# Spatial gate's value rows projected in one pass of 512 columns, with weights loaded two inner tiles at a time and split by VectorE

## The chip, the cores and the metric

The kernel runs on one core of one Trainium2 chip. The time is device microseconds (us) of that core from launch to end; the median of three runs is quoted, and one more execution was recorded by the hardware profiler. PE is the matrix engine (TensorE), DVE is VectorE, ACT is ScalarE, POOL is GpSimd, SP is the engine that issues most loads.

## What is computed

One layer of a diffusion backbone over 1,280 tokens (1,024 latent and 256 context) of width 1,024. A modulated RMSNorm `u` of the tokens is projected by `w_in` into the inputs of three branches (pooling, spatial gating, a bidirectional mLSTM with four heads) and their gates; the gated branches are merged, projected out, and a feed-forward part follows. The change touches the branch with the spatial gate:

```python
proj = u @ w_in
xp, su, sv, q, k, v, o_pre, gate_pre, br_pre = jnp.split(proj, points, axis=-1)
y_b = sgu_branch(su, sv, g_sgu, w_sgu, b_sgu)

def sgu_branch(u, v, g_sgu, w_sgu, b_sgu):
    B, T, _ = u.shape
    vn = rmsnorm(v, g_sgu).reshape(B, T // CHUNK, CHUNK, N_SGU_GROUPS, SGU_GROUP)
    mixed = jnp.einsum('gpq,bnqgc->bnpgc', w_sgu, vn) + jnp.swapaxes(b_sgu, 0, 1)[None, None, :, :, None]
    return u * mixed.reshape(B, T, D_SGU)
```

`sv` (1,280 rows of 512 columns) is `u` times 512 columns of `w_in`; each row is normalised by its own root mean square over the 512 columns.

## The kernel before

**Matrix products.** Every operand is held as two rounded parts, `hi` and `lo` (`hi` is a rounded copy made by ACT, `lo` is the rest, made by a subtraction), and a product is three matmuls: hi·hi, lo·hi, hi·lo. `uT[k][g]` holds the transposed `u` for inner tile k (8 tiles of 128) and token group g (512, 512 and 256 tokens).

**The spatial rows (`sv`, lines 685 to 707).** For these, tokens are the output rows: the stationary operand is 128 tokens of `uT`, the moving operand is the weight. The 512 columns are done in two halves `q` of 256. For each half, `load_w` fetches two tiles `[128, 1024]` (four inner tiles by 256 columns each), ACT rounds them (line 93) and, with `eng=G`, POOL subtracts (line 94). Then ten token tiles `i` follow, each 8 × 3 matmuls of 256 columns into half of a bank `ps_mm`; ACT copies the result into `vn[i]` (line 701) and takes its sum of squares (line 702) into `vsq`. After both halves the two sums are added (line 704), `rstd_of` makes the inverse root (a DVE and a POOL instruction, lines 129 and 130), and DVE scales the ten `vn` (line 707).

**What stands around it.** A scheduler orders all instructions by its own estimate of time; the engines then run their queues in that order. In that order the `sv` matmuls lie between the steps of the last two heads of the mLSTM (`head(2)`, `head(3)`): a head's group of chunks goes through `st` and `rb` (lines 627, 631), DVE and ACT build the weights `w` and `e` (lines 635 to 645), PE multiplies them into `pv` (lines 654, 656), ACT and DVE normalise (lines 659 to 670) and PE transposes back (`th`, line 671). Groups are numbered 0, 1, 2 within a head. Each head's output gate `p_o` uses the same three banks `ps_mm` as `sv` and is read out by ACT on line 617.

**After `sv`** come the pooling branch and the rest of the spatial branch: `pool_project` (`p_xp`), `pool_window` (sums over windows on DVE and POOL, lines 758 to 776, in regions of the tile `z` that the last head uses until its `pv` is done), `pool_out` (`pp`, line 783), and `spatial(ci)`: ten matmuls `mx` of `vn` (line 831), `mt` on DVE (line 835), a projection `p_su`, and the product of both on DVE (line 842), which is what frees a bank of `p_su`.

**Pools.** `raw` has 2 buffers of `[128, 1024]`, `hi` and `lo` 3 each (`NRAW`, `NHL`), `ps_mm` 3 banks, `ps_sd` 5 banks, `slot` 59 tiles of `[128, 512]`.

Of the kernel before, what the change touches and what calls it, by code (L numbers as in the profile page):

```python
# [7 lines left out]
F32 = mybir.dt.float32  # L8
F32R = mybir.dt.float32r
AF = mybir.ActivationFunctionType  # L10
ALU = mybir.AluOpType
# [3 lines left out]
P = 128  # L15
D = 1024
KT = D // P
NSAMP = 1024
T = 1280
NT = T // P  # L20
# [8 lines left out]
NTMP, NRAW, NHL = 5, 2, 3  # L29
# [19 lines left out]
def hybrid_step(  # L49
# [8 lines left out]
    V, A, G, PE = engines  # L58
# [6 lines left out]
    wp = pw.enter_context(tc.tile_pool(name="wp", bufs=NRAW))  # L65
# [3 lines left out]
    def slot(name, dt=F32R):  # L69
        return sp.tile([P, 512], dt, tag="s", name=name)  # L70
# [4 lines left out]
    def ps_mm(name):  # L75
        return pp.tile([P, 512], F32, tag="mm", name=name, bufs=3)
# [4 lines left out]
    def small(shape, name, bufs=4):  # L81
        return cp.tile(shape, F32, tag=f"sm{shape[-1]}", name=name, bufs=bufs)

    def fetch_w(src, name):
        raw = wp.tile([P, 1024], F32, tag="raw", name=f"raw_{name}")
        SP.dma_start(raw, src)
        return raw

    def load_w(src, name, raw=None, eng=V):
        raw = fetch_w(src, name) if raw is None else raw  # L90
        hi = wp.tile([P, 1024], F32R, tag="hi", name=f"hi_{name}", bufs=NHL)
        lo = wp.tile([P, 1024], F32R, tag="lo", name=f"lo_{name}", bufs=NHL)
        A.copy(hi, raw)
        eng.tensor_tensor(lo, raw, hi.bitcast(F32), ALU.subtract)
        return hi, lo
# [10 lines left out]
    def split_part(name, g):  # L106
        if g < 2:
            return slot(f"{name}h{g}"), slot(f"{name}l{g}")
        c = slot(f"{name}c")
        return c[:, 0:256], c[:, 256:512]  # L110
# [16 lines left out]
    def rstd_of(ssq, n, name):  # L127
        r = small([P, 16], f"rs_{name}")
        V.tensor_scalar(r[:, :n], ssq, 1.0 / n_of[name[0]], EPS, ALU.mult, ALU.add)  # L129
        G.tensor_tensor(r[:, :n], r[:, :n], neghalf[:, :n], ALU.pow)  # L130
        return r
# [89 lines left out]
    uT = [[] for _ in range(KT)]  # L221
# [54 lines left out]
    V, A, G, PE = (Pinned(tc, e) for e in engines)  # L276
# [119 lines left out]
    for at, (g, k) in enumerate(steps):  # L396
# [3 lines left out]
        if (g, k) == (1, 2):  # L400
# [4 lines left out]
            for i in range(2):  # L405
                w = slot(f"wgs{i}").rearrange("p (k c) -> p k c", c=P)
# [25 lines left out]
    V, A, G, PE = engines  # L432
# [251 lines left out]

    vn = []
    vsq = cp.tile([P, NT, 2], F32, name="vsq")
    for q in range(2):
        wq = [load_w(w_sv[q, hf], f"sv{q}_{hf}", eng=G) for hf in range(2)]
        for i in range(NT):
            g, o = (i * P) // 512, (i * P) % 512  # L690
            if q == 0:
                vn.append(slot(f"vn{i}", F32))
            ps = ps_mm(f"sv{q}_{i}")
            for k in range(KT):
                whi, wlo = wq[k // 4]
                s = slice((k % 4) * 256, (k % 4 + 1) * 256)
                uh, ul = uT[k][g]
                PE.matmul(ps[:, :256], uh[:, o : o + P], whi[:, s], start=k == 0, stop=False)
                PE.matmul(ps[:, :256], ul[:, o : o + P], whi[:, s], start=False, stop=False)
                PE.matmul(ps[:, :256], uh[:, o : o + P], wlo[:, s], start=False, stop=k == KT - 1)  # L700
            A.copy(vn[i][:, q * 256 : (q + 1) * 256], ps[:, :256])
            A.activation(ps[:, 256:512], ps[:, :256], AF.Square, accum_out=vsq[:, i, q : q + 1])
    vs1 = small([P, 16], "vs1")[:, :NT]
    V.reduce_sum(vs1, vsq, axis=mybir.AxisListType.X)
    r = rstd_of(vs1, NT, "v")
    for i in range(NT):
        V.tensor_scalar(vn[i], vn[i], r[:, i : i + 1], None, ALU.mult)
# [179 lines left out]
    def tmp2(name, dt=F32):  # L887
        return q1.tile([P, 512], dt, tag="s", name=name, bufs=6)
# [156 lines left out]
    for ri, r in enumerate(ORDER):  # L1045
        scr = (scr_ya, scr_yb, scr_yc)[r]
        ys = [[] for _ in range(4)]
        for g in range(3):
            for kc in range(4):
                t0, n = GROUPS[g]  # L1050
                raw = tmp2(f"yr{r}_{kc}_{g}")
                SP.dma_start(raw[:, :n], scr[kc, :, t0 : t0 + n])
                hi, lo = split_part(f"y{r}_{kc}", g)
# [3 lines left out]
        for d in range(KT):  # L1057
            if d % 2 == 0:
                wb = [load_half(w_branch[r, d // 2][:, i * 512 : i * 512 + 512], f"wb{r}_{d}_{i}") for i in range(2)]
            for g in range(3):  # L1060
# [4 lines left out]
                for kc in range(4):  # L1065
                    yh, yl = ys[kc][g]
                    whi, wlo = wb[kc // 2]
                    o = kc % 2 * 256 + (d % 2) * P
                    s = slice(o, o + P)
# [230 lines left out]
    for j in range(2):  # L1300
        for hf in range(2):
            t = q2.tile([P, 512], F32, name=f"gt2{j}{hf}")
# [152 lines left out]
def _layout(inputs):  # L1455
    import numpy as np

    f = {k: np.asarray(v) for k, v in inputs.items()}
    a = {}
    a["xs"] = np.concatenate([f["x_sample"][0], f["x_prompt"][0]], 0).reshape(NT, P, D)  # L1460

    def col(v, n):
        return v.reshape(n, P).T

    cond = np.stack([f["c"][0], f["c_ctx"]], -1).reshape(KT, P, 2).transpose(1, 0, 2).reshape(P, 16)
    a["cols"] = np.concatenate(
        [
            cond, col(f["b_ada"][0, :2048], 16), col(f["g_norm1"][0], 8), col(f["g_norm2"][0], 8),
            col(f["pool_scale"][0], 4), col(f["g_sgu"][0], 4), col(f["g_mlstm"][0], 4),
        ], 1)  # L1470
    s = np.arange(P)
    neg = np.float32(-1e30)
    a["consts"] = np.concatenate(
        [
            np.eye(P, dtype=np.float32),
            np.where(s[:, None] <= s[None, :], np.float32(0), neg),
            np.where(s[:, None] >= s[None, :], np.float32(0), neg),
            np.tile(np.eye(2, dtype=np.float32), (64, 1)),
        ], 1).astype(np.float32)
    sel = np.zeros((100, 8), np.float32)  # L1480
    for d in range(2):
        for h in range(H):
            sel[32 * d + h, 4 * d + h] = 1.0
            sel[64 + 32 * d + h, 4 * d + h] = 1.0
    a["sel8"] = sel
    a["w_ada"] = f["w_ada"][0]
    a["b_ada"] = f["b_ada"]
    w = f["w_in"][0]
    wd = np.concatenate([w[:, :1024], w[:, 1536:3584], w[:, 3600:]], 1)
    a["w_in"] = wd.reshape(KT, P, 48, P).transpose(2, 1, 0, 3).reshape(48, P, KT * P)  # L1490
    a["w_sv"] = w[:, 1024:1536].reshape(2, 4, P, 2, 256).transpose(3, 0, 2, 1, 4).reshape(2, 2, P, 1024)
    wgt = np.zeros((KT, P, P), np.float32)
    wk = w[:, 3584:3600].reshape(KT, P, 16)
    bg = np.zeros((36, 2), np.float32)
    m0 = np.zeros((36, 1), np.float32)
    for t in range(2):
        for d in range(2):
            j = t * 8 + d * 4
            for o in (0, 4):
                wgt[:, :, 64 * t + 32 * d + o : 64 * t + 32 * d + o + 4] = wk[:, :, j : j + 4]  # L1500
            bg[32 * d : 32 * d + 4, t] = f["b_gates"][0, j : j + 4]
    for d in range(2):
        m0[32 * d : 32 * d + 4, 0] = f["state_m"][0, 0, d]
    a["w_gate"] = wgt.transpose(1, 0, 2)
    a["bg"], a["m0"] = bg, m0
    a["w_branch"] = f["w_branch"][0].reshape(3, 4, P, 4, 256).transpose(0, 3, 2, 1, 4).reshape(3, 4, P, 1024)
    a["w_out"] = f["w_out"][0].reshape(KT, P, 2, 512).transpose(2, 0, 1, 3)
    a["w_ff1"] = f["w_ff1"][0].reshape(KT, P, NFF, P).transpose(2, 1, 0, 3).reshape(NFF, P, D)
    a["w_ff2"] = f["w_ff2"][0].reshape(NFF, P, D)
    a["w_pool"] = f["w_pool"][0].transpose(1, 0, 2)  # L1510
    a["w_sgu"] = f["w_sgu"][0].transpose(2, 0, 1)
    a["b_sgu"] = f["b_sgu"][0].reshape(1, 4 * P)

    def inv(n, win):
        t = np.arange(n)
        cnt = np.clip(t + win - win // 2, 0, n) - np.clip(t - win // 2, 0, n)
        return (np.float32(1.0) / cnt.astype(np.float32)).astype(np.float32)

    a["pcnt"] = np.stack([
        np.concatenate([np.outer(inv(GRID_H, w_), inv(GRID_W, w_)).ravel(), inv(256, w_)]) for w_ in POOL_WINDOWS])  # L1520
    st = np.concatenate([f["state_C"][0, 0], f["state_n"][0, 0][..., None]], -1)
    a["state"] = st.transpose(1, 2, 0, 3)
    a["gfin"] = f["g_final"].reshape(1, D)
    return {k: np.ascontiguousarray(v) for k, v in a.items()}
# [31 lines left out]
```

## Time and profile before

| | us |
|---|---|
| median of three runs (lowest, highest) | 1944.16 (1943.91, 1946.34) |
| the profiled execution's own time | 1943.31 |
| its span, first to last instruction | 1941.3 |
| PE busy | 1908.4 (98%) |
| DVE busy | 1287.9 (66%) |
| ACT busy | 856.7 (44%) |
| POOL busy | 382.1 (20%) |

The span is what the trace covers; the time adds what lies around it. Busy shares are means over the whole span. A PE that counts as busy can still be slower than it could be, since matmuls overlap and what counts is the distance from one start to the next. Where PE is idle, the views name the engine and line that released it.

### The profile page before, as it was taken

Reading aid. Unit: us, or ns where it says so; the run is one execution under the profiler, and the core shown is the slowest. Engines: PE = TensorE matmul, PEld = TensorE weight load, DVE = VectorE, ACT = ScalarE, POOL = GpSimd, SP = SyncE. Lnnn points to the kernel's source line nnn. Section 1 sums busy time; section 2 is a strip of 40 time slices with the busy share of each in tenths; the row PEclk is TensorE's granted clock in tenths of the full one; section 3 lists DMA queues with packets and bytes.
Section 4 is the critical chain, followed back from the end, with each engine's and each line's share of the span. In section 5 each row is a group of like instructions: output and inputs, shape, how many; then the busy total and the mean of one; then the engine's idle time right before and its main releaser. Section 6 shows DMA issues by size and latency. Waiting matters only on the chain.

```text
span 1941.3 us, 28162 instructions
## 1 busy us (share of the span) xinstructions
PE 1908.4 (98%) x10166; PEld 1632.5 (84%) x10166; DVE 1287.9 (66%) x2200; ACT 856.7 (44%) x1760; POOL 382.1 (20%) x381
## 2 busy tenths in 40 slices
PE   8999999999999999999999999999999999999998
PEld 5878888998788888888888888888888888888886
DVE  6574443447759899875675599887876655754665
ACT  6444454653243333343123375555454544443443
POOL 1100001108202424230000005554431210000003
PEclk9999999999999999999999999999999999999999
DMA  9210111012635445459532435777774596654444
GB/s 370 77 60 33 45 38 39 28 57 68 204 125 168 151 151 161 157 195 328 164 103 98 151 121 200 275 263 264 250 256 139 193 335 203 210 168 152 165 133 160
DMA packets 149318, 313.33 MB, mean 161 GB/s; under 512 B 17550, under 2 KB 40818, under 8 KB 147130
## 3 DMA queue, kind: packets, MB, share of 16 engines
q1 hardware_dynamic: 107354, 220.73, 34.6%
q0 software_dynamic: 15520, 57.75, 7.8%
q10 hardware_dynamic: 26304, 33.04, 4.7%
q8 instruction: 80, 1.31, 0.3%
q14 instruction: 60, 0.49, 0.1%
HBM read 217.59 MB, written 93.36 MB: 160 GB/s over the span
## 4 chain that ended last, share of the span: by engine, by line
PE 87%; DVE 6%; ACT 2%; issue 2%; DMA 2%; POOL 1%; SPq 0%; ACTq 0%; POOLq 0%; DVEq 0%
PE w L1423 6%; PE w L1424 6%; PE w L1425 6%; PE fT L912 3%; PE fT L910 3%; PE fT L911 3%; PE pb L1071 3%; PE pb L1070 3%; PE pb L1072 3%; PE fB L911 2%; PE fB L910 2%; PE fB L912 2%; PE fT_g L912 2%; PE fT_g L910 2%; PE fT_g L911 2%; PE po L1190 2%
## 5 line engine op out<-in xcount | busy, mean ns | idle before, releaser
L1262 POOL TENSOR_TENSOR z<-z 128x512 f32<-128x512 f32 x64 | 100.6, 1572 | 119.6 <-DMA z<-in_w_ff 110.1
L967 DVE TENSOR_TENSOR z<-z 128x512 f32<-128x512 f32 x112 | 94.2, 841 | 2.5
L547 POOL PARTITION_ALL_REDUCE acc<-acc x16 | 54.4, 3435 | 183.4 <-DVE acc L541 114.3
L541 DVE SCALAR_TENSOR_TENSOR acc<-z,scond,acc 128x512 f32<-128x512 f32 x112 | 84.6, 803 | 0.1
L1377 POOL TENSOR_TENSOR rs_y<-rs_y,neghalf 128x1 f32<-128x1 f32 x10 | 9.7, 967 | 332.2 <-DVE rs_y L1376 332.1
L1228 ACT ACTIVATE z<-z 128x512 f32<-128x512 f32 x64 | 40.5, 632 | 75.7 <-DVE z L976 38.4
L992 ACT ACTIVATE z<-z 128x512 f32<-128x512 f32 x48 | 30.3, 632 | 54.2 <-DVE z L976 20.6
L130 POOL TENSOR_TENSOR rs_h<-rs_h,neghalf 128x4 f32<-128x4 f32 (+1 forms) x12 | 10.9, 909 | 200.0 <-DVE rs_h L129 199.8
L673 DVE SCALAR_TENSOR_TENSOR yc<-th,ccol,z 128x512 f32<-128x512 f32 (+1 forms) x12 | 7.9, 661 | 58.4 <-PE th L671 58.4
L1076 DVE TENSOR_TENSOR sg<-pb,sg 128x512 f32<-128x512 f32 (+1 forms) x48 | 28.8, 601 | 26.6 <-PE pb L1072 26.4
L901 ACT CAST hi_wb<-raw_wb 128x512 fp32r<-128x512 f32 x24 | 14.7, 620 | 64.0 <-PE pb L1071 37.9
L1229 ACT ACTIVATE z<-z 128x512 f32<-128x512 f32 x64 | 40.3, 629 | 1.1
L1191 DVE TENSOR_TENSOR po<-po,gt 128x512 f32<-128x512 f32 (+1 forms) x24 | 14.6, 609 | 35.6 <-PE po L1190 31.2
L548 POOL TENSOR_TENSOR acc<-acc,bt 1x512 f32<-1x512 f32 x16 | 26.2, 1651 | 59.1 <-issue 59.1
L1253 POOL DMA_DIRECT2D scr_s<-x x48 | 26.3, 550 | 52.4 <-DVE x L1247 46.6
L758 POOL TENSOR_TENSOR z<-z 128x1024 f32<-128x1024 f32 (+13 forms) x20 | 33.6, 1702 | 7.7 <-ACT z L742 5.4
L1194 ACT ACTIVATE po<-z 128x512 f32<-128x512 f32 (+1 forms) x24 | 12.7, 530 | 48.6 <-DVE z L1193 34.3
L607 DVE SCALAR_TENSOR_TENSOR z<-z,dmb,kv 128x129 f32<-128x129 f32 x56 | 16.6, 345 | 21.8 <-PE kv L596 21.3
L1077 DVE TENSOR_TENSOR z<-z,sg 128x512 f32<-128x512 f32 (+1 forms) x48 | 28.7, 602 | 1.2
L660 DVE TENSOR_TENSOR den<-den,gcol 128x2 f32<-128x2 f32 x40 | 6.2, 160 | 31.0 <-ACT den L659 29.9
L130 POOL TENSOR_TENSOR rs_f<-rs_f,neghalf 128x4 f32<-128x4 f32 (+1 forms) x3 | 3.3, 1092 | 116.9 <-DVE rs_f L129 116.9
L654 PE MATMUL pv<-z,w 128*128 128x129 f32 x160 | 25.1, 275 | 0.9 <-DVE w L638 0.9
(5142 smaller groups left out, 7274.1 us busy)
## 6 DMA issues: line engine op xcount, KB each, us to landing
z<-in_w_ff SPq DMA_DIRECT2D x64, 512.0 KB, 5.3
z<-in_w_ada SPq DMA_DIRECT2D x64, 256.0 KB, 3.4
scr_t<-z POOLq DMA_DIRECT2D x16, 1024.0 KB, 4.3
z<-in_w_in SPq DMA_DIRECT2D x24, 512.0 KB, 4.3
scr_g<-z ACTq DMA_DIRECT2D x48, 256.0 KB, 2.0
sg<-scr_g SPq DMA_DIRECT2D x48, 256.0 KB, 4.5
scr_h<-z ACTq DMA_DIRECT2D x48, 256.0 KB, 3.5
scr_s<-x POOLq DMA_DIRECT2D x48, 256.0 KB, 3.8
```

The costliest lines, as they stand in the source:

```text
L541: V.scalar_tensor_tensor(acc[j], raw, scond[:, k, j : j + 1], acc[j], ALU.mult, ALU.add)
L910: PE.matmul(ps, whi[:, s], ahi, start=first and k == ks[0], stop=False)
L911: PE.matmul(ps, whi[:, s], alo, start=False, stop=False)
L912: PE.matmul(ps, wlo[:, s], ahi, start=False, stop=end and k == ks[-1])
L967: V.tensor_tensor(out, x, y, op)
L1070: PE.matmul(pb[:, :n], whi[:, s], yh, start=kc == 0, stop=False)
L1071: PE.matmul(pb[:, :n], whi[:, s], yl, start=False, stop=False)
L1072: PE.matmul(pb[:, :n], wlo[:, s], yh, start=False, stop=kc == 3)
L1262: G.tensor_tensor(out, x, y, ALU.subtract)
L1423: PE.matmul(banks[j], h_[:, s], rh, start=fp == 0, stop=False)
L1424: PE.matmul(banks[j], l_[:, s], rh, start=False, stop=False)
L1425: PE.matmul(banks[j], h_[:, s], rl, start=False, stop=fp == NFP - 1)
```

## The change

The 512 columns are done in one pass. There are four loads of the same size as before, but each holds two inner tiles by 512 columns; each half of a load is rounded by ACT and subtracted by DVE in an instruction of its own (512 columns). The first three loads keep `hi` and `lo` tiles of the pool of weights (all three buffers of each); the fourth puts its four parts into `slot` tiles. Each token tile is 24 matmuls of 512 columns into a whole bank, one copy and one sum of squares, which goes straight to `vs1`; the addition on line 704 is gone.

```diff
-    for q in range(2):
-        wq = [load_w(w_sv[q, hf], f"sv{q}_{hf}", eng=G) for hf in range(2)]
-        for i in range(NT):
-            g, o = (i * P) // 512, (i * P) % 512
-            if q == 0:
-                vn.append(slot(f"vn{i}", F32))
-            ps = ps_mm(f"sv{q}_{i}")
-            for k in range(KT):
-                whi, wlo = wq[k // 4]
-                s = slice((k % 4) * 256, (k % 4 + 1) * 256)
-                uh, ul = uT[k][g]
-                PE.matmul(ps[:, :256], uh[:, o : o + P], whi[:, s], start=k == 0, stop=False)
-                PE.matmul(ps[:, :256], ul[:, o : o + P], whi[:, s], start=False, stop=False)
-                PE.matmul(ps[:, :256], uh[:, o : o + P], wlo[:, s], start=False, stop=k == KT - 1)
-            A.copy(vn[i][:, q * 256 : (q + 1) * 256], ps[:, :256])
-            A.activation(ps[:, 256:512], ps[:, :256], AF.Square, accum_out=vsq[:, i, q : q + 1])
-    vs1 = small([P, 16], "vs1")[:, :NT]
-    V.reduce_sum(vs1, vsq, axis=mybir.AxisListType.X)
+    vs1 = vsq[:, :, 0]
+    wsv = []
+    for j in range(4):
+        raw = fetch_w(w_sv[j], f"sv{j}")
+        for kk in range(2):
+            rk = raw[:, kk * 512 : kk * 512 + 512]
+            if j < 3:
+                if kk == 0:
+                    whole = [wp.tile([P, 1024], F32R, tag=t, name=f"{t}_sv{j}", bufs=NHL) for t in ("hi", "lo")]
+                hi, lo = (t[:, kk * 512 : kk * 512 + 512] for t in whole)
+            else:
+                hi, lo = slot(f"hi_sv{j}{kk}"), slot(f"lo_sv{j}{kk}")
+            A.copy(hi, rk)
+            V.tensor_tensor(lo, rk, hi.bitcast(F32), ALU.subtract)
+            wsv.append((hi, lo))
+    for i in range(NT):
+        g, o = (i * P) // 512, (i * P) % 512
+        vn.append(slot(f"vn{i}", F32))
+        ps = ps_mm(f"sv{i}")
+        for k in range(KT):
+            whi, wlo = wsv[k]
+            uh, ul = uT[k][g]
+            PE.matmul(ps, uh[:, o : o + P], whi, start=k == 0, stop=False)
+            PE.matmul(ps, ul[:, o : o + P], whi, start=False, stop=False)
+            PE.matmul(ps, uh[:, o : o + P], wlo, start=False, stop=k == KT - 1)
+        A.copy(vn[i], ps)
+        A.activation(ps, ps, AF.Square, accum_out=vs1[:, i : i + 1])
```

The host lays the weights out to match (four tiles of two inner tiles by 512 columns). From line 714 on, a line of the kernel before has a number larger by 9 in the changed one (758 is 767, 776 is 785, 831 is 840, 835 is 844, 842 is 851). The scheduler's order differs from head 2's last weight roundings up to the first gate products; outside of that stretch it is the same.

**ACT, from head 2's group 1.** The old rows are marked -, the new ones +; `w_1_0` and `e_1_0` are the weights of that group, `sv` the first token tile's bank.

```order
 L617 ACTIVATE z<-p_o_3512 128x512
-L93 CAST hi_sv_0_4053<-raw_sv_0_4051 128x1024
+L699 CAST hi_sv_3777<-raw_sv_3775 128x512
 L637 ACT_TABLE_LOAD
 L637 ACTIVATE w_1_0_2911<-w_1_0_2911 128x512
 L643 ACTIVATE e_1_0_2918<-rb_1_0_2909,dmb 128x128 x4
+L699 CAST hi_sv_3777<-raw_sv_3775 128x512
 L637 ACTIVATE w_1_1_2926<-w_1_1_2926 128x512
 L643 ACTIVATE e_1_1_2933<-rb_1_1_2924,dmb 128x128 x4
-L701 COPY vn_3771<-sv_0_3772 128x256
+L712 COPY vn_3793<-sv_3794 128x512
```

One rounding of 1,024 columns ahead of the exponentials became two of 512, one ahead of them and one between them.

**DVE, behind head 3's last group.** First the rows before, from the last scaled `vn` on, then those of the changed kernel from its last `vn` on.

```order
L707 TENSOR_SCALAR vn_4023<-vn_4023,rs_v 128x512
L673 SCALAR_TENSOR_TENSOR yc_2_3755<-th_2_3750,ccol,z 128x256
L758 TENSOR_TENSOR z<-z 128x1920
L94 TENSOR_TENSOR lo_xp_4789<-raw_xp_4786,hi_xp_4788 128x1024
L758 TENSOR_TENSOR z<-z 128x1792
L758 TENSOR_TENSOR z<-z 128x1536
L758 TENSOR_TENSOR z<-z 128x1024
L765 TENSOR_TENSOR z<-z 128x1024
L776 TENSOR_TENSOR xp_0_4382<-z,xp_0_4382 128x512
```

```order
L716 TENSOR_SCALAR vn_4045<-vn_4045,rs_v 128x512
L673 SCALAR_TENSOR_TENSOR yc_2_3755<-th_2_3750,ccol,z 128x256
L94 TENSOR_TENSOR lo_su_4655<-raw_su_4652,hi_su_4654 128x1024
L767 TENSOR_TENSOR z<-z 128x1920
L844 SCALAR_TENSOR_TENSOR mt_0_4408<-mx_0_4403,ccol,z 128x512
L844 SCALAR_TENSOR_TENSOR mt_1_4415<-mx_1_4410,ccol,z 128x512
L844 SCALAR_TENSOR_TENSOR mt_2_4420<-mx_2_4417,ccol,z 128x256
L767 TENSOR_TENSOR z<-z 128x1792
L851 TENSOR_TENSOR mt_0_4408<-mt_0_4408,p_su_4428 128x512
L767 TENSOR_TENSOR z<-z 128x1536
L851 TENSOR_TENSOR mt_1_4415<-mt_1_4415,p_su_4455 128x512
L767 TENSOR_TENSOR z<-z 128x1024
```

The `mt` work of the first spatial group, which stood behind the window sums of the first pooling group, now stands among them.

**PE, at the same place.** Before, head 3's last transposes are followed by 114 matmuls of `p_xp` and then the first `mx`; now by 18 of `p_xp` and 19 of `p_su`. The last rows ahead of `mx`, the `mx` rows' first and the rows of `pp`, before and then now:

```order
L671 MATMUL th_2_3750<-cst,z 128x128 x2
L123 MATMUL p_xp_4471<-u2h_737,hi_xp_4440 128x512
...
L125 MATMUL p_xp_4613<-u7c,lo_xp_4556 128x256
L831 MATMUL mx_0_4665<-z,vn_3771 128x128
...
L783 MATMUL pp_0_4771<-xp_0_4382,z 128x512
```

```order
L671 MATMUL th_2_3750<-cst,z 128x128 x2
...
L840 MATMUL mx_0_4403<-z,vn_3793 128x128
...
L840 MATMUL mx_2_4417<-z,vn_4045 128x128
...
L792 MATMUL pp_0_4509<-xp_0_4120,z 128x512
L792 MATMUL pp_1_4514<-xp_1_4147,z 128x512
```

Between head 3's last `pv` and the first `mx` PE now has 40 and 18 matmuls of `p_xp` and 19 of `p_su`, against 49 and 114 of `p_xp`; between the last `mx` and the first `pp` it has 53 of `p_su` and 27 of `p_xp`, against 72 of `p_su`.

## Rows read from the trace of the kernel before

**Rows 1.** The page: busy time of each engine, and the first line of the chain of work that ended last.
```profile
PE 1908.4 (98%) x10166; PEld 1632.5 (84%) x10166; DVE 1287.9 (66%) x2200; ACT 856.7 (44%) x1760; POOL 382.1 (20%) x381
PE 87%; DVE 6%; ACT 2%; issue 2%; DMA 2%; POOL 1%; SPq 0%; ACTq 0%; POOLq 0%; DVEq 0%
```

**Rows 2.** PE's waits between 320 and 500 us: who waited for whom, us in total, times, longest. A wait counts from the modelled end of the last matmul.
```profile
PE sv L698 <- ACT sv L702: 1.2, 1, 1.2
PE p_xp L123 <- DVE mt L842: 1.1, 1, 1.1
PE pv L654 <- DVE w L638: 0.9, 1, 0.9
```

**Rows 3.** Timeline of PE inside `sv`: start, duration, line. Ten rows are left out between the two.
```profile
402.81 0.28 PE L698 MATMUL sv<-hi_sv,u6h 128*128 128x256 f32 x1
...
404.12 0.28 PE L700 MATMUL sv<-lo_sv,u1h 128*128 128x256 f32 x1
```

**Rows 4.** The same in the projection out, which has tokens stationary and 512 weight columns moving. Eleven rows are left out between the two.
```profile
1059.79 0.39 PE L1189 MATMUL po<-hi_wo,m0l 128*128 128x512 f32 x1
...
1062.51 0.39 PE L1189 MATMUL po<-hi_wo,m4l 128*128 128x512 f32 x1
```

**Rows 5.** Timelines of ACT, DVE and PE in head 2's group 1.
```profile
343.07 1.05 ACT L93 CAST hi_sv<-raw_sv 128x1024 fp32r<-128x1024 f32 x1 [0.82 <-PE p_o L124]
...
345.97 1.13 ACT L643 ACTIVATE e<-rb,dmb 128x128 f32<-128x128 f32 x4
...
346.10 0.69 DVE L638 TENSOR_TENSOR w<-w,st 128x512 f32<-128x512 f32 x1 [2.16 <-ACT w L637]
...
346.93 0.46 PE L654 MATMUL pv<-z,w 128*128 128x129 f32 x2 [0.90 <-DVE w L638]
```

**Rows 6.** Timeline of PE at the start of the third token tile, and of ACT where `p_o` of group 1 is read out.
```profile
355.13 0.39 PE L698 MATMUL sv<-hi_sv,u0h 128*128 128x256 f32 x1 [1.22 <-ACT sv L702]
...
360.38 0.60 ACT L617 ACTIVATE z<-p_o 128x512 f32<-128x512 f32 x1
```

**Rows 7.** Instructions of single lines: count, duration in ns (least, median, most), first and last start, shape. Line 727 is the plain copy of a bank of 512 columns; 809 and 810 are a rounding and a subtraction of 512 columns.
```profile
L93 ACT CAST hi_sv<-raw_sv x4: 1047/1048/1062, 304.8 to 383.1; 128x1024 fp32r<-128x1024 f32 x4
L94 POOL TENSOR_TENSOR lo_sv<-raw_sv,hi_sv x4: 2380/2396/2402, 306.0 to 384.2; 128x1024 fp32r<-128x1024 f32 x4
L94 DVE TENSOR_TENSOR lo_xp<-raw_xp,hi_xp x3: 1224/1225/1226, 386.8 to 427.4; 128x1024 fp32r<-128x1024 f32 x3
L727 ACT COPY xp<-p_xp x12: 364/586/590, 431.8 to 505.0; 128x512 f32<-128x512 f32 x8, 128x256 f32<-128x256 f32 x4
L809 ACT CAST T4h<-z x4: 608/610/625, 521.7 to 542.0; 128x512 fp32r<-128x512 f32 x4
L810 DVE TENSOR_TENSOR T4l<-z,T4h x4: 684/688/692, 524.8 to 542.7; 128x512 fp32r<-128x512 f32 x4
```

**Rows 8.** Timeline of PE: head 3's last `pv`, the first `mx`, the first `pp`, and the `p_xp` that waits.
```profile
438.79 0.83 PE L654 MATMUL pv<-z,w 128*128 128x129 f32 x6
...
470.24 2.40 PE L831 MATMUL mx<-z,vn 128*128 128x128 f32 x20
...
486.27 2.31 PE L783 MATMUL pp<-xp,z 128*128 128x512 f32 x6
...
489.72 0.50 PE L123 MATMUL p_xp<-u0h,hi_xp 128*128 128x512 f32 x1 [1.14 <-DVE mt L842]
```

**Rows 9.** Timeline of DVE behind head 3: the scaling of the ten `vn`, then the first pooling group's window.
```profile
446.63 11.80 DVE L707 TENSOR_SCALAR vn<-vn,rs_v 128x512 f32<-128x512 f32 x10 [1.85 <-POOL rs_v L130]
458.36 0.47 DVE L673 SCALAR_TENSOR_TENSOR yc<-th,ccol,z 128x256 f32<-128x256 f32 x1
458.75 2.14 DVE L758 TENSOR_TENSOR z<-z 128x1920 f32<-128x1920 f32 x1
...
461.95 5.91 DVE L758 TENSOR_TENSOR z<-z 128x1792 f32<-128x1792 f32 x3
...
470.89 3.42 DVE L776 TENSOR_TENSOR xp<-z,xp 128x512 f32<-128x512 f32 x2
```

**Rows 10.** Timeline of POOL over the same time.
```profile
443.89 2.71 POOL L130 TENSOR_TENSOR rs_v<-rs_v,neghalf 128x10 f32<-128x10 f32 x1
446.56 8.63 POOL L758 TENSOR_TENSOR z<-z 128x1216 f32<-128x1216 f32 x5
...
466.75 8.05 POOL L758 TENSOR_TENSOR z<-z 128x1120 f32<-128x1120 f32 x4
```

**Rows 11.** Timeline of DVE later: a product that frees a bank of `p_su`, and pooling sums of a later group at a time with less POOL work.
```profile
480.67 1.79 DVE L835 SCALAR_TENSOR_TENSOR mt<-mx,ccol,z 128x512 f32<-128x512 f32 x3
...
488.99 0.67 DVE L842 TENSOR_TENSOR mt<-mt,p_su 128x512 f32<-128x512 f32 x1
...
495.40 1.22 DVE L765 TENSOR_TENSOR z<-z 128x1024 f32<-128x1024 f32 x1
496.54 0.41 DVE L842 TENSOR_TENSOR mt<-mt,p_su 128x256 f32<-128x256 f32 x1
496.87 1.50 DVE L776 TENSOR_TENSOR xp<-z,xp 128x512 f32<-128x512 f32 x2
```

**Rows 12.** Stretches: start and end, length, busy us of PE, PEld, DVE, ACT and POOL with their instruction counts, granted clock of PE as a share of its full speed, DMA share, GB/s.
```profile
128.00:131.00 3.00, 0.00 (x0) 0.00 (x0) 2.85 (x6) 0.00 (x0) 1.07 (x2) 1.00 0.00 0
131.00:138.00 7.00, 6.38 (x35) 5.95 (x36) 6.92 (x22) 2.70 (x4) 0.00 (x0) 0.51 0.05 12
```

More of the change, by code (lines that the diff above doesn't have):

```diff
@@ L1490, in _layout @@
     a["w_in"] = wd.reshape(KT, P, 48, P).transpose(2, 1, 0, 3).reshape(48, P, KT * P)
-    a["w_sv"] = w[:, 1024:1536].reshape(2, 4, P, 2, 256).transpose(3, 0, 2, 1, 4).reshape(2, 2, P, 1024)
+    a["w_sv"] = w[:, 1024:1536].reshape(4, 2, P, 512).transpose(0, 2, 1, 3).reshape(4, P, 1024)
     wgt = np.zeros((KT, P, P), np.float32)
```

## The prediction

> **What bounds the kernel now.** I read the page first: PE is busy for 98% of the span and carries 87% of the chain that ended last [rows 1]. So a change is worth what it takes from PE's own work, plus or minus the holes between matmuls. The view of waits then gives PE's holes in the stretch that the change reorders, 320 to 500 us. There are three, 3.2 us together [rows 2]: the third token tile of `sv` waits for ACT to empty its bank, the first `pv` of head 2's group 1 waits for the weight `w`, and a `p_xp` waits for a bank that DVE has not yet freed. All else there hides behind PE.
>
> **The wide pass, −2.8 us.** 480 matmuls of 256 columns become 240 of 512. PE's price is the distance between starts, not the duration. Narrow ones: eleven steps from 402.81 to 404.12, 0.119 us each [rows 3]. Wide ones of the very same form (tokens stationary, weights moving) stand in the projection out: twelve steps from 1059.79 to 1062.51, 0.2267 us [rows 4]. So 480 × 0.119 = 57.2 against 240 × 0.2267 = 54.4: two narrow ones cost 0.238, one wide one 0.227.
>
> The Trainium skill (TensorE: Matmul & The Clock Gate, section on the back-to-back issue gap) gives the spacing of isolated warm matmuls as columns over 2.4 GHz plus about 2.5 ns, and says that small ones cost more in a stream with weight loads. By that formula 256 and 512 columns would be 109 and 216 ns and the term 0.6 us, an estimate from the page; both rows lie above it, the narrow one by more, as its caveat says, and the rows are used.
>
> **Weights and evictions, 0.** ACT rounds eight times 0.61 instead of four times 1.05 us, 0.7 more; DVE takes on eight subtractions of 0.69, 5.5 us; POOL loses four of 2.40 [rows 7]. DVE is free for a third of the span [rows 1], and what counts is only where they stand in its queue: six of them stand ahead of the `sv` matmuls, beside `p_q` and `p_o`, and the last two in head 2's group 1 (below). Without the cover one costs 0.7 us. Emptying a bank takes 0.59 for the copy [rows 7], and about 0.6 for the squares by the same width, plus 0.2 for the sum, half as often as before. The line 704 addition was off the path. All three `hi` buffers are now held until the last token tile, so the first pooling weights are rounded only when its first two inner tiles are through: 1.05 + 1.23 = 2.3 us [rows 7], against 18 wide matmuls that are left of that tile, 4.1 us, and 16 `pv` instructions beside them. Without that cover it would cost 2.3.
>
> **Head 2's two waits, 2.1 to 0.9, so −1.2 us.** Group 1's order on ACT was: rounding of 1.05 us from 343.07, table load, exponentials; its `w` came from DVE at 346.8 and PE went on at 346.93 [rows 5]. Now the first rounding is 0.61, so `w` comes 0.44 earlier, at about 346.4 (the DVE subtraction beside it ends before the exponential does). PE now has 15 wide matmuls ahead of it, 3.4 us from about 343.0, when the rounding was let go: it arrives at 346.4 as well, and the 0.9 is gone. The second rounding now stands behind the first exponentials `e`, which ended at 347.1 [rows 5] and will at 346.7; done at 347.3, it is asked for about 0.3 earlier. The other wait is of banks. `p_o` of groups 1 and 2 keeps two of three until ACT reads it at 360.38 [rows 6], so `sv` has one, and each tile waits for its predecessor's eviction; before, the third tile waited 1.2 [rows 6]. Now the second tile has all of group 1's `pv` ahead of it and needn't wait; the third has only the transposes, `st` and `rb`, about 1 us, against an eviction of 1.4 to 1.6: some 0.6 is left. Together 0.9. Bounds: 0, if the eviction is hidden; 2.6, if both the weights' rounding and each eviction come out a microsecond late.
>
> **The wait at 489, −1.1 us.** There `p_xp` waited for a bank that a `mt` product on DVE freed late, at 488.99, behind window sums [rows 8, 11]. In the new order 27 matmuls of `p_xp` follow `p_su`, and the first such product stands behind one sum only; by the count below it is about 2 us ahead of PE. If not, up to 1.1 stays.
>
> **A new wait at the first `pp`, +1.5 us.** Filler has moved: `sv` and `p_xp` run between head 3's steps, and little is left behind its last `pv`, on whose end the pooling windows wait, as their region of `z` is the head's. Take that `pv` as zero (438.79 before [rows 8]). On PE, `mx` comes after about 1.3 of `pv`, 34 wide and 24 narrow of `p_xp`, and 19 wide `p_su`: 1.3 + 7.7 + 2.9 + 4.3 = 16.2 (before: 31.5). Its `vn`: POOL finished the inverse root at +7.8 [rows 10], now up to 0.9 earlier, since nothing of DVE is in its way. The ten scalings took 11.8 us, as five POOL sums took turns with them [rows 9, 10]; two of these five now come earlier, so about 10.2. The fourth `vn` is then ready at about +15, the last at +17.6, when PE needs it at about +18: no wait, but little room. DVE goes on: 0.47 + 1.23 + 2.14 + 1.79 [rows 7, 9, 11] brings it to +23.2. From there to the second `xp` took 12.4 us before, from 461.95 to 474.3 with POOL sums in the way [rows 9, 10], and three `mt` products come on top, 1.75 [rows 11]: +37.3. With POOL out of the way, at 1.2 us per 1,024 columns [rows 11], it would be +32.9. PE gets to `pp` with 2.2 of `mx`, 56 wide and 24 narrow: 16.2 + 2.2 + 12.7 + 2.9 = +34.0, and to the second `pp` 0.9 later. So the wait is 0 to 2.4; POOL has the next group's sums to do at that time, as before, so I take 1.5. The later windows fall behind 72 `p_su` and have room.
>
> **Sum.** −2.8 − 1.2 − 1.1 + 1.5 = −3.6 us. The profiled execution took 1943.31, 0.85 less than the median of 1944.16; the sum is a difference and goes on the median: 1940.6. What a measurement of this kernel can tell from no change is about 0.2%, 3.9 us, so this lies at that border.
>
> **Rivals.**
> *No new wait* (0.12). POOL stays clear of DVE in that stretch, and ACT empties banks in time: −2.8 − 2.1 − 1.1 = −6.0, 1938.2. For it: the sums without POOL cost little more than half [rows 9, 11]. Against: POOL was at work in it before.
> *The gain goes back at `pp`* (0.16). DVE comes 2 us later still: +3.5 there, net −1.6, 1942.6. For it: little room at `mx`, since every delay of the `vn` moves all that follows.
> *The wide pass saves nothing* (0.05), that is, the change doesn't do what it says: if PE's price went by the columns alone, the first term would be 0 and the time 1943.4. The rows speak against it: 0.119 is more than half of 0.2267 [rows 3, 4]. The Trainium skill's formula (TensorE: Matmul & The Clock Gate, back-to-back issue gap) goes that way: with its 0.6 instead of 2.8 the time would be 1942.8, an estimate from that page.
> *A long hole and a slow clock* (0.07), the slower side. After 3 us without a matmul the granted clock was 0.51 for the next 7 us, 1.2 GHz instead of 2.4 [rows 12], which costs about 3.4 us. If the second `xp` came only at +40, PE would stand for 5.1 us in one piece: −2.8 − 1.2 − 1.1 + 5.1 + 3.4 = +3.4, and from +40.5 on the kernel is slower by over 0.2%. That takes 3 us more than the chain above, with POOL in the way already.
>
> **How the numbers follow.** My forecast, net −2.2 to −5.2, has 0.60: 1940.6, its own range 1939.0 to 1942.0. Faster by over 0.2% is about half of it and *no new wait*: 0.32 + 0.12 = 0.44. Slower is 0.07. The rest, 0.49, is within 0.2%. The range for 8 in 10 reaches to *no new wait* and to the net of about zero: 1937.8 to 1944.2.
>
> **What would show it.** Right: 240 `sv` matmuls at 0.227 from start to start; PE's wait for `w` in head 2 gone; one short wait of `sv` for line 713; none at the first `p_xp` behind `p_su`; a wait of 1 to 2 us of `pp` for line 785. Wrong: a pitch other than 0.227; `mx` waiting for `vn`; `p_xp` waiting for the roundings on line 93 at the end of `sv`; or a stretch of PE with a granted clock of half. A gap that opens later, in the gate products, would be one that I don't see now: DVE's splits there stand behind the same window sums.

## The result, and the profile after

The changed kernel takes 1946.83 us (median; 1944.43 to 1950.25) against 1944.17 for the kernel before in the same comparisons: ratio 1.0015, 95% interval 1.0008 to 1.0022. So it is slower by 2.7 us (interval 1.6 to 4.3): the median lies within the 0.2% (3.9 us) that the prediction called no change, and outside its range of 1937.8 to 1944.2. The profiled execution took 1944.43, with a span of 1942.7.

PE has 240 matmuls fewer, and the steps in `sv` are as forecast, yet it is busy as long as before [rows 1]. The page's line, and the timeline of PE inside a token tile of `sv` (start, duration, line; ten rows left out), where eleven steps from 351.93 to 354.43 are 0.227 us each:

```profile
PE 1908.9 (98%) x9926; PEld 1620.3 (83%) x9926; DVE 1295.7 (67%) x2207; ACT 854.7 (44%) x1734; POOL 372.6 (19%) x377
```

```profile
351.93 0.39 PE L710 MATMUL sv<-hi_sv,u1l 128*128 128x512 f32 x1
...
354.43 0.39 PE L709 MATMUL sv<-hi_sv,u5h 128*128 128x512 f32 x1
```

Between 320 and 500 us PE now waits for nothing at all; all three waits of [rows 2] are gone. But behind 500, where the kernel before has no wait up to the gate products, there are three. PE's waits in the changed kernel, 500 to 560 us:

```profile
PE p_su L123 <- DVE mt L851: 4.3, 1, 4.3
PE pp L792 <- DVE mt L844: 1.0, 1, 1.0
PE mx L840 <- ACT ya L794: 1.0, 1, 1.0
```

The timeline of PE there, and the stretches (start and end, length, busy us and instructions of PE, PEld, DVE, ACT, POOL, granted clock, DMA share, GB/s):

```profile
515.93 1.98 PE L792 MATMUL pp<-xp,z 128*128 128x512 f32 x4 [1.03 <-DVE mt L844]
522.18 0.80 PE L123 MATMUL p_su<-u0h,hi_su 128*128 128x512 f32 x1 [4.26 <-DVE mt L851]
522.78 0.63 PE L124 MATMUL p_su<-u0l,hi_su 128*128 128x512 f32 x1
523.20 0.63 PE L125 MATMUL p_su<-u0h,lo_su 128*128 128x512 f32 x1
...
525.45 0.39 PE L125 MATMUL p_su<-u2h,lo_su 128*128 128x512 f32 x1
```

```profile
521.00:525.20 4.20, 3.02 (x7) 2.42 (x8) 3.62 (x6) 1.21 (x2) 0.00 (x0) 0.59 0.95 312
525.20:530.00 4.80, 4.01 (x26) 3.44 (x24) 4.56 (x9) 1.50 (x3) 0.00 (x0) 1.00 0.29 111
```

The first `p_su` of the third spatial block stands for 4.3 us, and then PE runs at half its clock, 1.2 GHz: the steps are 0.42 to 0.43 us until 525 and 0.23 again behind it. The seven steps from 522.18 to 525.22 take 3.0 us, where 1.6 would do: 1.4 us are lost.

A measure that is free of what happens elsewhere in an execution is the stretch from the first `sv` matmul to the first gate product: 215.6 us before, 217.9 after. Up to the second block's first `p_su` it gained 6.5 (163.2 to 156.7: 2.7 of pitch, 2.4 of head 2's holes, 1.4 at 489), and from there on it lost 8.8 (52.4 to 61.2): the waits of 4.3, 1.0 and 1.0, which in steps from start to start are holes of 4.6, 1.3 and 1.2, and 1.4 of clock, 8.5 of the 8.8.

**Why that `p_su` waits.** Its bank was `p_su`'s of the second block, which DVE frees with the product on line 851. DVE's timeline in the changed kernel, then the same product and the same `p_su` before (842 there):

```profile
480.62 2.97 DVE L774 TENSOR_TENSOR z<-z 128x1024 f32<-128x1024 f32 x1
...
491.58 1.23 DVE L94 TENSOR_TENSOR lo_su<-raw_su,hi_su 128x1024 fp32r<-128x1024 f32 x1 [4.53 <-ACT hi_su L93]
...
508.99 3.41 DVE L785 TENSOR_TENSOR xp<-z,xp 128x512 f32<-128x512 f32 x2
...
513.35 0.74 DVE L844 SCALAR_TENSOR_TENSOR mt<-mx,ccol,z 128x512 f32<-128x512 f32 x1
...
518.51 1.22 DVE L774 TENSOR_TENSOR z<-z 128x1024 f32<-128x1024 f32 x1
...
520.24 1.28 DVE L785 TENSOR_TENSOR xp<-z,xp 128x512 f32<-128x512 f32 x2
521.45 0.68 DVE L851 TENSOR_TENSOR mt<-mt,p_su 128x512 f32<-128x512 f32 x1
```

```profile
514.78 0.68 DVE L842 TENSOR_TENSOR mt<-mt,p_su 128x512 f32<-128x512 f32 x1
```

```profile
523.50 0.79 PE L123 MATMUL p_su<-u0h,hi_su 128*128 128x512 f32 x1
```

In both kernels the product stands in DVE's queue behind the sums of windows 1 and 0, the last two. Before, it was done 8 us ahead of PE (514.78 + 0.68 against 523.50). Now PE is 6 us earlier (it would start at about 517.4) and the product 6.7 later.

**Why DVE is later.** Head 3 ends later: its last `pv` begins at 451.92 instead of 438.79 [rows 8], since 158 matmuls of `p_xp` stand ahead of it instead of 53. That is PE's own queue: the 105 more are 62 of 512 columns and 43 of 256, 19.2 us at 0.2267 and 0.119, and 19.2 less the 2.7 of pitch and the 2.4 of head 2's holes is 14.1, where the trace has 14.4 (from the first `sv` matmul, 110.2 against 95.8). The windows' sums lie in the piece of `z` that head 3 uses, and DVE has the ten scalings of `vn` to do at that point. Timelines of PE, DVE, SP's queue and POOL:

```profile
451.92 0.61 PE L654 MATMUL pv<-z,w 128*128 128x129 f32 x4
```

```profile
459.01 10.34 DVE L716 TENSOR_SCALAR vn<-vn,rs_v 128x512 f32<-128x512 f32 x10 [2.67 <-POOL rs_v L130]
469.28 0.47 DVE L673 SCALAR_TENSOR_TENSOR yc<-th,ccol,z 128x256 f32<-128x256 f32 x1
```

```profile
470.14 0.43 SPq L743 DMA_DIRECT2D z<-in_pcnt  x1
```

```profile
475.50 1.70 POOL L778 TENSOR_TENSOR z<-z 128x256 f32<-128x256 f32 x1 [9.19 <-DMA z<-in_pcnt]
...
479.42 10.57 POOL L767 TENSOR_TENSOR z<-z 128x1120 f32<-128x1120 f32 x6
```

POOL then waits 9.2 us for the reciprocal counts of the first window, whose load stands in SP's queue behind head 3's last store, and DVE 4.5 us at 487 for what POOL and ACT do next.

ACT is slower too in one of head 3's steps, from `rb` to the first weight `w`. Its timeline before, then after:

```profile
393.41 0.63 ACT L637 ACTIVATE w<-w 128x512 f32<-128x512 f32 x1
```

```profile
400.33 0.59 ACT L712 COPY vn<-sv 128x512 f32<-128x512 f32 x1 [2.24 <-DVE w L635]
...
402.83 0.63 ACT L637 ACTIVATE w<-w 128x512 f32<-128x512 f32 x1
```

Before, `w` starts 1.7 us behind the first `rb` (391.7); after, 4.2 us behind it (398.7): the emptying of a bank of 512 columns stands ahead of the table load. But no matmul between 320 and 500 us waits for it, so it did not hold PE up; whether a slower step is why the scheduler put the filler there was not tried.

### The profile page after: what moved, and what is told of

Same layout as the page of the kernel before. It is cut to its first block, busy times and chain, and to the rows that moved or that the text cites. A ratio compares the mean times of both kernels' runs of the same rounds, so it can differ in the third digit from the quotient of the medians.

```text
span 1942.7 us, 27652 instructions
## 1 busy us (share of the span) xinstructions
PE 1908.9 (98%) x9926; PEld 1620.3 (83%) x9926; DVE 1295.7 (67%) x2207; ACT 854.7 (44%) x1734; POOL 372.6 (19%) x377
## 4 chain that ended last, share of the span: by engine, by line
PE 54%; DVE 3%; issue 1%; DMA 1%; ACT 1%; POOL 0%; ACTq 0%; POOLq 0%; SPq 0%; DVEq 0%
PE w L1432 6%; PE w L1433 6%; PE w L1434 6%; PE fT L921 3%; PE fT L919 3%; PE fT L920 3%; PE pb L1080 3%; PE pb L1079 3%; PE pb L1081 3%; PE fB L919 2%; PE fB L920 2%; PE fB L921 2%; PE po L1197 2%; PE po L1199 2%; PE po L1198 2%; PE fc L919 2%
## 5 line engine op out<-in xcount | busy, mean ns | idle before, releaser
L767 POOL TENSOR_TENSOR z<-z 128x256 f32<-128x256 f32 (+13 forms) x20 | 34.4, 1733 | 5.8 <-ACT z L752 3.8
L1083 DVE TENSOR_TENSOR z<-pb,sg 128x512 f32<-128x512 f32 (+1 forms) x24 | 14.2, 598 | 18.2 <-PE pb L1081 18.2
```

## The experiments

Stretch: first `sv` matmul to first gate product, from each kernel's trace. The ratio is to the kernel before, whose medians beside these runs were 1944.17 to 1944.62.

| kernel | median us | ratio (95%) | stretch us |
|---|---|---|---|
| before | 1944.17 | | 215.6 |
| changed | 1946.83 | 1.0015 (1.0008 to 1.0022) | 217.9 |
| e1_mt_ahead | 1942.80 | 0.9990 (0.9980 to 0.9999) | 212.8 |
| e2_pinv_early | 1950.25 | 1.0031 (1.0021 to 1.0041) | 223.0 |
| e3_split_pool | 1949.85 | 1.0027 (1.0017 to 1.0037) | 219.7 |
| e4_before_mt_ahead | 1944.03 | 0.9999 (0.9990 to 1.0008) | 215.5 |
| e5_scale_act | 1942.86 | 0.9990 (0.9981 to 0.9999) | 212.2 |
| e6_mix_ahead | 1945.70 | 1.0005 (0.9996 to 1.0014) | 217.4 |
| e7_scale_mix | 1938.12 | 0.9966 (0.9952 to 0.9979) | 209.0 |
| e8_before_scale_act | 1941.35 | 0.9988 (0.9979 to 0.9996) | 213.8 |
| e9_before_scale_mix | 1942.36 | 0.9990 (0.9981 to 0.9999) | 213.8 |
| e10_scale_mix_pool | 1940.42 | 0.9980 (0.9971 to 0.9989) | 211.2 |
| e11_filler | 1947.54 | 1.0013 (1.0004 to 1.0022) | 220.0 |

**e1: the order on DVE alone.**

```diff
...
-            V.tensor_tensor(mix[g][:, :n], mix[g][:, :n], ps[:, :n], ALU.mult)
+            marks["mt", ci] = V.tensor_tensor(mix[g][:, :n], mix[g][:, :n], ps[:, :n], ALU.mult)
...
-    pool_window(0)
+    with tc.issue_after(marks["mt", 1].ins):
+        pool_window(0)
```

> The changed kernel, with one edit: DVE issues the window sums of pooling window 0 behind the three gating products (line 851) of the second spatial block instead of ahead of them; PE's order is untouched. Theory (the gain was lost because these products, which free the banks that the third block's p_su needs, stood behind two windows' worth of sums on DVE): the hole of 4.6 us ahead of that p_su (517.4 to 522.3) shrinks to 0 to 1.0 us, the 3.4 us at half the clock behind it vanish, so 4.0 to 6.3 us less than the changed kernel: 1940.5 to 1942.8, ratio to the kernel before 0.998 to 0.9993. Rival (DVE as a whole is late, and the order only decides where it shows): the hole reopens at the pp of window 0 or at the next mx, 4 us or more, and the time stays at 1946 to 1947. Second rival (the clock falls there for another reason than the hole): hole gone, half clock still there, about 1.7 us lost: 1942.5.

PE's waits from 500 to 540 us:

```profile
PE p_su L123 <- DVE mt L851: 2.1, 1, 2.1
PE pp L792 <- DVE mt L844: 1.0, 1, 1.0
```

The wait at `p_su` is halved (the product comes at 520.05, as it now stands behind quarter sums that wait for a load), the clock stays at 1.00 and the `mx` no longer waits: 1942.8, the upper end of the theory, with a larger hole left than the 0 to 1.0 us expected. So at least half of the hole is due to where the product stands, and the slow clock goes with the larger hole.

**e4: the same edit on the kernel before.** 

> The kernel before with the edit of the first run: the gating products of the second spatial block ahead of window 0's sums on DVE. Theory (there PE comes 6 us later and does not wait for these products, so nothing is to be had): within 0.1% of the kernel before, 1943 to 1945.5. Rival (the order of DVE is a fault of its own, whatever the change): 2 us or more faster, 1942 or less.

As the theory said, nothing: 0.9999. This order on DVE costs only a PE that comes early.

**e2: the counts loaded early.** Three `slot` tiles take the first window's counts; `pinv3` stands for `pinv` in `pool_window(3)`.

```diff
...
+    pinv3 = [slot(f"pinv3_{g}", F32) for g in range(3)]
+    for t, (t0, n) in zip(pinv3, GROUPS):
+        SP.dma_start(t[:, :n], pcnt[3:4, t0 : t0 + n].partition_broadcast(P))
     pool_project(3)
```

> The changed kernel, with one edit: the reciprocal counts of the first pooling window lie in three slots of their own and are loaded during head 3, instead of in the piece of z that head 3 still uses, so that POOL need not wait for them (9.2 us until 475.5). DVE multiplies in two instructions instead of one. Theory (the whole chain of windows is late because head 3 now ends 12.5 us later on PE and the counts' load stands behind its last store): POOL's wait goes, DVE's idle 4.5 us at 487 to 491.6 goes, the product of line 851 comes at about 517 instead of 521.45, the hole ahead of the third p_su is 0 to 0.7 us and the half clock goes: 1940.5 to 1942, ratio 0.998 to 0.999. Rival (DVE's own load sets the time of that product: scalings, sums and splits without a gap): POOL's wait moves elsewhere, the product comes less than 1.5 us earlier, a hole of 3 us or more is left, 1945 to 1947.

POOL's wait (460 to 480 us), PE's (460 to 500), and two rows of ACT's timeline:

```profile
POOL z L778 <- DMA z<-in_pcnt: 8.2, 1, 8.2
```

```profile
PE p_su L123 <- DVE mt L851: 5.3, 1, 5.3
PE p_su L123 <- ACT xp L736: 3.7, 1, 3.7
```

```profile
487.01 0.62 ACT L751 COPY z<-xp 128x512 f32<-128x512 f32 x1 [18.95 <-POOL z L767]
487.54 0.85 ACT L736 COPY xp<-p_xp 128x512 f32<-128x512 f32 x2
```

It did not test what it should: POOL went on and then waited 8.2 us for the counts of the next window, which still go to `z`. And the scheduler changed the order of more than the sums: on ACT the two copies that empty the last `p_xp` banks ahead of `p_su` now stand behind a copy for a later window, which waits 19 us for POOL. They start at 487.54, where the changed kernel has them at 461.18 and 465.09. With two of the three banks full, the first block's second `p_su` waits 5.3 us for its first product (476.29), and its third one 3.7 us for ACT; the granted clock behind the two waits was 0.50 (477 to 480.5 us) and 0.54 (487 to 494.5). Nothing follows for the load, nor for the order on DVE; it is one more case of a bank that is freed late because what frees it stands behind window work, here on ACT.

**e5: the chain on DVE made shorter.**

```diff
-        V.tensor_scalar(vn[i], vn[i], r[:, i : i + 1], None, ALU.mult)
+        A.activation(vn[i], vn[i], AF.Copy, scale=r[:, i : i + 1])
```

> The changed kernel, with one edit: the ten scalings of vn (line 716, 10.3 us on DVE ahead of everything that follows head 3) are done by ACT. Apart from them DVE's, POOL's and PE's order stay as they are. Theory (the windows, and the gating products behind them, are late because their whole chain hangs on the end of head 3 and on DVE's queue there): yc of line 673 comes at about 462 instead of 469.3, the counts' load and POOL's sums 7 us earlier, the product of line 851 at about 514 instead of 521.45, ahead of PE's 517.4. The holes of 4.63 and 1.29 us and the 3.4 us at half the clock are gone, about 7.5 us less than the changed kernel: 1938 to 1941, ratio 0.997 to 0.9985. Rival (POOL and the transfers set the time of the windows, not DVE): the product comes less than 3 us earlier, a hole of 2 us or more is left, 1943 to 1946.5. Other rival (ACT gets in the way: evictions of p_xp behind the scalings): a new wait of p_xp for line 736 near 462.

The product on DVE and the `p_su` on PE, then PE's wait (500 to 560 us) and one of ACT's (510 to 560):

```profile
515.78 0.67 DVE L851 TENSOR_TENSOR mt<-mt,p_su 128x512 f32<-128x512 f32 x1
```

```profile
516.51 0.50 PE L123 MATMUL p_su<-u0h,hi_su 128*128 128x512 f32 x1
```

```profile
PE mx L840 <- ACT ya L794: 2.4, 2, 1.7
```

```profile
ACT ya L794 <- DMA scr_yb<-mt: 2.5, 1, 2.5
```

With DVE's order untouched but 10.3 us taken out of its queue, the product comes 5.7 us earlier, PE reaches `p_su` 5.7 earlier without a wait, and the clock holds. So it is the chain behind head 3 that was late. Of the 7.5 us expected 4.0 came (5.7 in the stretch), and 1942.86 lies above the range of 1938 to 1941: behind the closed hole `mx` waits 2.4 for ACT, whose `ya` stands behind stores.

**e6: more of the order on DVE**, on top of e1: `spatial(1)` ahead of `pool_window(1)` in the code, the latter issued behind line 844's last instruction of that block, and `quarter_sums` behind its products. 

> The changed kernel, with DVE's order alone edited further than in e1_mt_ahead: the mixing of the second spatial block (line 844) ahead of window 1's sums, its products (line 851) ahead of window 0's sums and of the quarter sums. PE's order is untouched. Theory: in e1_mt_ahead 1.29 us (pp for line 844) and 2.42 us (p_su for line 851, itself behind quarter sums that wait for a load) were left of the hole; with the bank freed at about 505 and the product at about 511 both go, and pp of window 1 waits 0 to 1.5 us instead. 2 to 4 us less than e1_mt_ahead: 1939 to 1941, ratio 0.997 to 0.9985. Rival (what is given to the products is taken from the windows, as both need DVE): pp of window 1 or of window 0 waits 2.5 us or more, no gain on e1_mt_ahead: 1942.5 to 1944.

PE's wait, 500 to 560 us, and DVE's, 510 to 560:

```profile
PE mx L840 <- ACT ya L794: 5.4, 2, 3.6
```

```profile
DVE z L809 <- DMA z<-scr_u: 9.4, 2, 7.8
```

The product came at 513.30 and the hole went, but two others opened 8 us behind it and later, in another place than either side had said: a quarter sum ahead of window 0 in DVE's queue waits 7.8 us for its load, ACT's casts wait for it, the `ya` behind these casts, and `mx` for `ya`, with a granted clock of 0.50 behind it (528 to 531.5 us). 1945.7 is 2.9 us more than e1, above both ranges.

**e7: e5 and e6 together.** 

> Both edits of e5_scale_act and e6_mix_ahead on the changed kernel. Theory: once the chain is early, the order no longer matters, so it lies within 0.8 us of the better of the two: 1938 to 1940.5. Rival (the two cure different waits): 2 us or more below the better one.

PE's waits from 320 to 560 us are down to one:

```profile
PE fB_g L924 <- DVE a_g0l L905: 0.4, 1, 0.4
```

1938.12: the rival was right, the two edits cure different waits. It beats the kernel before by 6.2 us and the changed one by 8.7.

**e8: the scalings on ACT in the kernel before.** 

> The kernel before with the scalings of vn on ACT. Theory (there only the wait of p_xp for a product of line 842 at 488 hangs on this chain, 1.1 us with some gap behind it): 0.5 to 1.5 us less than before, 1942.8 to 1944, ratio 0.999 to 1.0. Rival (DVE's queue costs the kernel before as much as the changed one): 4 us or more less.

The wait of `p_xp` at 488 goes; 1941.35 is 3.0 us below the median before, with an interval from 0.8 to 4.1 us faster. The stretch shows 1.8 us. Both are more than the theory's 0.5 to 1.5.

**e9: the kernel before with both edits.** 

> The kernel before (narrow passes, split by POOL) with both edits of e7_scale_mix. Theory (the pass and the split are worth what the prediction's first terms and head 2's waits say, as soon as nothing behind them gives it back: 2.8 of pitch and 2.4 of waits): with the late chain cured on both sides the kernel before is 4 to 6.5 us slower than e7_scale_mix. Its wait at 488 goes as in e8, nothing else: 1940.5 to 1943, ratio 0.998 to 0.9995. Rival (e7's gain is that of the two edits and the wide pass brings nothing): within 1.5 us of e7_scale_mix, 1937 to 1939.5.

1942.36, so the change is worth 4.2 us once nothing behind it gives the gain back (4.8 in the stretch). The two waits in head 2 are still there in e9 and gone in e7.

**e3 and e10: only the split undone**, on the changed kernel and on e7: `G.tensor_tensor(lo, …)` in place of `V.tensor_tensor(lo, …)`.

> The changed kernel with only its second half undone: the low parts of the sv weights are subtracted by POOL as before, the pass is still one of 512 columns. The order of DVE behind head 3 is the same as in the changed kernel. Theory (the pass alone moves head 3's end, and the split is hidden): 1945.8 to 1947.8, the hole of 4 to 5 us ahead of the third block's p_su and the half clock are there. Rival (the split on VectorE is what makes DVE late): the hole is gone or below 2 us, 1941 to 1944.

> e7_scale_mix with the low parts of the sv weights subtracted by POOL again (the second half of the change undone, nothing else behind head 2 moves). Theory (of the 2.4 us that head 2 gains some 1.4 to 1.6 come from the split, as e3_split_pool has a bank wait of sv of 1.6 us that the changed kernel does not have): 1.4 to 2 us slower than e7_scale_mix, 1939.5 to 1941. Rival (the split costs nothing either way, and the wait in e3_split_pool came from something else): within 0.6 us of e7_scale_mix.

PE's waits from 320 to 560 us, PE's and ACT's timeline in `sv`, and the stretch behind the hole, of e3:

```profile
PE p_su L123 <- DVE mt L851: 4.0, 1, 4.0
PE sv L709 <- ACT sv L713: 1.5, 2, 1.4
PE pp L792 <- DVE mt L844: 1.0, 1, 1.0
PE mx L840 <- ACT ya L794: 0.5, 1, 0.5
```

```profile
350.60 0.48 PE L711 MATMUL sv<-lo_sv,u7h 128*128 128x512 f32 x1
352.44 0.50 PE L709 MATMUL sv<-hi_sv,u0h 128*128 128x512 f32 x1 [1.36 <-ACT sv L713]
```

```profile
351.20 0.59 ACT L712 COPY vn<-sv 128x512 f32<-128x512 f32 x1
```

```profile
523.00:530.00 7.00, 6.56 (x19) 5.32 (x20) 5.51 (x10) 2.19 (x4) 0.00 (x0) 0.57 0.54 198
```

The hole is there with either split, so it is the pass that brings it. The split has a worth of its own: 2.3 us between e10 and e7 (2.2 in the stretch), and without it a bank wait of 1.4 us is there, now of the second token tile. PE's order differs: a half of a load takes POOL 1.29 us, where DVE takes 0.68, and with POOL the first tile's last matmul (350.60) stands behind all 32 `pv` of head 2's group 1, so that the second tile follows it at once and waits for its bank. In the changed kernel that matmul starts at 348.55, and 20 of the `pv` run while ACT empties the bank. e3 at 1949.85 is 2 us above what was expected, with that wait and a half clock twice as long.

**e11: filler moved back.** Pieces of `p_xp` are told to follow given instructions of head 3 (`rb` of group 1 from step 8, `pv` of group 1 from 18, `rb` of group 2 from 32, `pv` of group 2 from 42; a step is three matmuls). The code is written out for these pieces, so 851 is 866 here.

```diff
...
+                after = [key for key, at in BEHIND if step >= at]
...
+                    with tc.issue_after(marks[after[-1]].ins):
+                        dense(ps, w, uT, g, (k,))
```

> The changed kernel with PE's order edited in head 3: of the 158 p_xp matmuls that stand ahead of its last pv, 23 are issued behind it (each later piece of p_xp must follow a given rb or pv of head 3), DVE and ACT as they are. The number of matmuls is the same. Theory (the filler that moved ahead of the end of head 3 takes the time that the windows' chain needs behind it): last pv about 5 us earlier, th_2 and yc about 3.4, the product of line 851 2 to 3.4 us earlier, so the hole ahead of the third p_su is 1 to 2.5 instead of 4.6, with no half clock behind it: 1941.5 to 1944.5. It may cost up to 2 us in waits of pv or th of head 3 for ACT, which would show there by name. Rival (where the filler stands does not matter, DVE's own queue decides): hole of 4 us or more as before, 1946 or more.

PE's waits from 320 to 560 us, DVE's timeline ahead of the second window, and a stretch behind the wait of `mx`:

```profile
PE p_su L123 <- DVE mt L866: 2.8, 1, 2.8
PE mx L855 <- ACT ya L809: 1.9, 1, 1.9
PE p_su L123 <- ACT xp L738: 1.6, 1, 1.6
```

```profile
485.79 0.41 DVE L866 TENSOR_TENSOR mt<-mt,p_su 128x256 f32<-128x256 f32 x1
491.99 1.63 DVE L782 TENSOR_TENSOR z<-z 128x1408 f32<-128x1408 f32 x1 [5.79 <-ACT z L787]
```

```profile
534.00:537.60 3.60, 3.60 (x10) 2.82 (x9) 2.64 (x5) 1.01 (x3) 0.00 (x0) 0.53 0.88 271
```

Inconclusive, and above the range of 1941.5 to 1944.5. Counted from the first `sv` matmul, the last `pv` came 3.2 us earlier, as 5 wide and 18 narrow matmuls are worth (3.3), and `yc` 2.6, but the product only 0.6 (179.2 against 179.8): DVE stood 5.8 us for ACT, and with it for POOL. The hole shrank to 2.8 mainly as PE came later itself, by a new wait of 1.6, and half the clock followed twice, behind the hole and behind the wait of `mx`. Nor was it a clean edit: 19 `p_su` that stood ahead of `mx` on PE, and single instructions on DVE and ACT, changed places too. So whether an earlier end of head 3 alone would close the hole stays open; 3.2 us of it did not.

## Why the prediction failed, point by point

**The wide pass, −2.8: right.** Steps of 0.227 against the row's 0.2267; 240 of them are 54.5 us against 57.2. e9 against e10, 1.9 us in the medians and 2.5 in the stretch, is this term and what is left of head 2's.

**Weights and evictions, 0: right as to waits**; no matmul waits for line 699. The split on DVE also lets the first tile end early enough for the second one's bank (e3).

**Head 2's two waits, −1.2: right in sign, too small.** Both are gone, 2.1 of wait and 2.4 in steps, where 0.9 was to stay: ahead of the third tile the transposes, `st` and `rb` took 1.4 us (356.49 to 357.92), where about 1 was reckoned, and ACT's emptying of the bank 1.2 (356.68 to 357.87), where 1.4 to 1.6 was.

**The wait at 489, −1.1: right**, gone with the gap of 0.3 beside it.

**The new wait at the first `pp`, +1.5: it did not come.** The count itself held: counted from the last `pv`, `mx` was forecast at +16.2 and came at +16.5, `pp` at +34.0 and came at +34.3, and the second `xp` came at +35.1, between the +32.9 and +37.3 of the two bounds. PE and DVE met within a microsecond, and no wait is recorded.

**The step that failed is the sentence behind it: "The later windows fall behind 72 `p_su` and have room."** It was not counted, and its number was at hand. Filler that moves ahead of the last `pv` is missing from all that follows, not only up to the first `pp`. Counted from the last `pv`, the `p_su` of the third block was due at +84.7 before (523.50 − 438.79) and is due at about +65.5 after; the 105 `p_xp` matmuls that moved are the 19.2 us between the two. The product on DVE was at +76.0 before (514.78 − 438.79) and came at +69.5: the chain of four windows is DVE's and POOL's own and shrinks little. Counted to the product's end, room of 8.0 us became a lack of 4.7. With 8.8 us there instead of 1.5 at `pp`, and 2.7, 2.4 and 1.4 for the other terms, the sum is +2.3, as measured in the stretch.

**The rivals.** *A long hole and a slow clock* had the mechanism and the sign, but at the first `pp` and at 0.07; it named 5.1 us of hole and 3.4 of clock, where the trace has 4.3 and 1.4, at a later meeting of PE and DVE. Its price came from a row of 3 us without a matmul [rows 12], which is part of a wait of 3.6 (until 131.62). *The wide pass saves nothing* is excluded by the steps. The list of what would show the forecast wrong had this stretch at half the clock, and looked for a later gap in the gate products; it opened 42 us ahead of them (517.9 against 559.6).

**The turns of DVE and POOL.** A sum of 1,024 columns took 1.22 us with POOL idle (line 774 at 518.51) and 2.97 beside POOL's sums (480.62). The Trainium skill (SBUF — State Buffer, section on who interferes with whom) says that a DVE instruction with two inputs in SBUF contends with a GpSimd one that reads SBUF; the trace agrees, as POOL was busy with sums from 479.42 to 489.99 and idle at 518.51. How much of DVE's later product is due to it was not tried by itself.

## What to carry to other kernels

When filler changes sides of an event that starts another engine's chain, count that chain to its end against PE's new arrival, at each place where the two meet; the first meeting may hold and a later one fail. An instruction that frees a bank can gain by standing in its queue ahead of work that nobody waits for yet (4.0 us in e1, nothing in e4), but each such move has to be followed through the queues behind it, as in e6 a load's wait took the hole's place. A gain in PE's own work shows only once what PE then runs into earlier has been moved as well: here 4.2 us of it came out in e7 against e9.

## What the runs showed of the hardware

Holes of about the same length were followed by slow stretches of different lengths. In the changed kernel PE stood for 4.3 us and the granted clock was half for 3.4 us (0.59 over 521 to 525.2), which cost 1.4; in e3 it stood for 4.0 and the clock was half for almost 7 (0.51 over 522 to 529), with twelve steps, most of 0.43 us, up to 528.7, which cost 2.5. Nor does the length of a wait tell whether the clock falls: in e1 one of 2.1 us left it at 1.00 (520 to 524), in e11 one of 2.8 was followed by 0.61 (523 to 527) and one of only 1.9 by 0.53 (534 to 537.6). So besides itself a hole cost nothing, about 1.5 us or about 2.5, and the rows of the kernel before did not tell which.
